# Turning the feed-forward activations on VectorE instead of TensorE

## The chip, the cores and the metric

The kernel runs on one core of one Trainium2 chip. The metric is the device time of one execution in microseconds (us), lower is better; the kernel before is given as the median of 3 executions. A core has TensorE (PE in the profile; PEld is its weight load), VectorE (DVE), ScalarE (ACT), GpSimd (POOL) and SyncE (SP), each with an instruction queue of its own, worked off in order.

## The reference, cut to what matters

The kernel computes one transformer layer for 256 latent tokens and 256 context tokens of width 2048: a modulated norm, a wide projection, two kinds of attention, an output projection, and a feed-forward part, all in float32. The change touches the last part alone:

```python
def swiglu_sublayer(x, shift, scale, gate, norm_g, w_ff_gate, w_ff_up, w_ff_down):
    h = modulate(rms_norm(x, norm_g), shift, scale)
    return x + gate * ((jax.nn.silu(h @ w_ff_gate) * (h @ w_ff_up)) @ w_ff_down)
```

The feed-forward width (DFF) is 5632 = 11 x 512.

## The kernel before

Every large product is made by one helper, `project`. It multiplies 256 tokens (two tiles `tk` of 128) by 512 weight columns and walks over the contraction in weight tiles of 2 x 128 rows. SyncE loads such a weight tile (`wraw`, 512 KB, seven buffers, L224). Float32 accuracy comes from splitting it into a rounded part and a rest: ScalarE casts it (`whi`, L231, three buffers), VectorE subtracts (`wlo`, L232, three buffers). TensorE then makes three matmuls for each of 2 x 2 pairs of row block and token tile (L236 with `whi`, L237 with `wlo`, L238 with `whi` and the rest of the activations): twelve matmuls of 512 columns a weight tile. `whi` and `wlo` of a tile can be made only when TensorE has finished the tile three before it.

`project` calls `tick()` and, if given, `side()` after every weight tile. `after(n, f)` puts `f` on a list that `tick()` counts down, so f runs some tiles later; `evac` is called when a token tile's sum is complete.

The feed-forward part has two stages. In gate/up, for each of 11 column groups `cg`, the gate projection (8 weight tiles) ends with a SiLU on ScalarE into `act[tk]`, and the up projection (8 more) ends with a multiplication into `act[tk]` on VectorE (L983, in place). The down stage multiplies `act` by `w_ff_down`, 22 weight tiles for each of 4 column groups. For that the activations have to stand transposed, as a split pair `fT`: TensorE turns `act[tk]` in four 128 x 128 pieces into PSUM (`ftp`, L990), then `split` casts (ScalarE, L241) and subtracts (VectorE, L242). From cg 2 on, two pieces of another vector (`ada`, L430/L432 on VectorE, 512 KB loaded each) are taken after each projection.

A scheduling layer settles the order of each queue when the program is built; the code gives the dependences and a first order.

Of the kernel before, what the change touches and what calls it, by code (L numbers as in the profile page):

```python
# [17 lines left out]
P = 128  # L18
D = 2048
NKT = D // P  # L20
# [14 lines left out]
CG = 512  # L35
# [5 lines left out]
TURN = 3  # L41
TURN2 = 5
# [3 lines left out]
def hybrid_block(ctx: ExitStack, tc: tile.TileContext, t: dict, out: bass.AP):  # L46
    nc = tc.nc
# [9 lines left out]
    def big_tile(name, dt=F32):  # L57
        return big.tile([P, 2048], dt, tag="big", name=name)

    def mm_ps(name="mm"):  # L60
        return psum.tile([P, CG], F32, tag="mm", bufs=4, name=name)

    def tp_ps(name="tp"):
        return psum.tile([P, CG], F32, tag="tp", bufs=2, name=name)
# [4 lines left out]
    def scratch(name, n=CG, dt=F32, tag="scr", bufs=3):  # L69
        return scr.tile([P, n], dt, tag=tag, bufs=bufs, name=name)  # L70
# [5 lines left out]
    ident = tab.tile([P, P], F32, name="ident")  # L76
# [145 lines left out]
    def load_w(src, r0, c0, nk=WK, in_big=False):  # L222
        raw = wp.tile([P, WK, CG], F32, tag="wraw", bufs=WRAW, name="wraw")
        nc.sync.dma_start(out=raw[:, 0:nk], in_=src[r0:r0 + nk * P, c0:c0 + CG].rearrange("(k p) c -> p k c", p=P))  # L224
        if in_big:
            both = big_tile("wbig", F32R).rearrange("p (h k c) -> p h k c", h=2, c=CG)
            hi, lo = both[:, 0], both[:, 1]
        else:
            hi = wp.tile([P, WK, CG], F32R, tag="whi", bufs=WHI, name="whi")
            lo = wp.tile([P, WK, CG], F32R, tag="wlo", bufs=WLO, name="wlo")  # L230
        last_hi.append(nc.scalar.copy(out=hi[:, 0:nk], in_=raw[:, 0:nk]))  # L231
        last_lo.append(nc.vector.tensor_tensor(out=lo[:, 0:nk], in0=raw[:, 0:nk], in1=hi[:, 0:nk].bitcast(F32), op=ALU.subtract))  # L232
        return hi, lo

    def mm3(ps, ah, al, wh, wl, first, last):
        nc.tensor.matmul(ps, lhsT=ah, rhs=wh, start=first, stop=False)  # L236
        nc.tensor.matmul(ps, lhsT=ah, rhs=wl, start=False, stop=False)  # L237
        return nc.tensor.matmul(ps, lhsT=al, rhs=wh, start=False, stop=last)  # L238

    def split(hi, lo, src):  # L240
        nc.scalar.copy(out=hi, in_=src)  # L241
        nc.vector.tensor_tensor(out=lo, in0=src, in1=hi.bitcast(F32), op=ALU.subtract)  # L242
# [178 lines left out]
    def ada_pieces(a, chunk):  # L421

        for kt, hf in [(kt, hf) for kt in range(NKT) for hf in range(2)]:
            wt = wp.tile([P, 1024], F32, tag="wraw", bufs=WRAW, name="wada2")
            nc.sync.dma_start(out=wt, in_=w_ada[kt * P:(kt + 1) * P, chunk * D + hf * 1024: chunk * D + (hf + 1) * 1024])
            dst = a[:, hf * 1024:(hf + 1) * 1024]
            yield None
            with tc.issue_after(last_lo[-1].ins):
                if kt == 0:
                    nc.vector.tensor_scalar(out=dst, in0=wt, scalar1=sc[:, 0, 0:1], scalar2=None, op0=ALU.mult)  # L430
                else:
                    nc.vector.scalar_tensor_tensor(out=dst, in0=wt, scalar=sc[:, 0, kt:kt + 1], in1=dst, op0=ALU.mult, op1=ALU.add)  # L432
# [94 lines left out]
    def take(gen, n):  # L527
        for _ in range(n):
            if next(gen, gen) is gen:
                return  # L530

    def drain(gen):
        for _ in gen:
            pass
# [9 lines left out]
    def after(n, fn):  # L544
        late.append([n, fn])

    def tick():
        for e in list(late):
            e[0] -= 1
            if e[0] <= 0:  # L550
                late.remove(e)
                e[1]()
# [61 lines left out]
    def project(src, hl, nkt, c0, evac, kt0=0, side=None, head=1, tail=1, hook=None):  # L614


        ps = [mm_ps() for _ in range(2)]
        nt = nkt // WK
        order = [(i, tk) for i in range(nt) for tk in range(2)]
        order[:2 * head] = [(i, tk) for tk in range(2) for i in range(head)]  # L620
        order[-2 * tail:] = [(i, tk) for tk in range(2) for i in range(nt - tail, nt)]
        wt = {}
        for n, (i, tk) in enumerate(order):
            if i not in wt:
                wt[i] = load_w(src, i * WK * P, c0, in_big=WHI <= i < head or nt - tail <= i < nt - WHI)
            wh, wl = wt[i]
            for j in range(WK):
                k = i * WK + j
                ah, al = hl.at(kt0 + k, tk * P, P)
                mm3(ps[tk], ah, al, wh[:, j], wl[:, j], k == 0, k == nkt - 1)  # L630
            if i == nt - 1 and (tail > 1 or tk == 1):
                for x in ([tk] if tail > 1 else range(2)):
                    evac(x, ps[x])
            if hook:
                hook(i, tk)
            if n % 2:
                tick()
                if side:
                    side()
                yield None  # L640
# [24 lines left out]
    def q_evac(qT, br):  # L665
        def f(tk, ps):
            o = norm_rope(ps, br, "q", tk)

            def turn():
                tp = tp_ps("qtp")  # L670
                for h in range(4):
                    nc.tensor.transpose(out=tp[:, h * P:(h + 1) * P], in_=o[:, h * P:(h + 1) * P], identity=ident)
                src = tp.rearrange("p (h q) -> p h q", h=4)
                split(qT[:, 0, :, tk * P:(tk + 1) * P], qT[:, 1, :, tk * P:(tk + 1) * P], src)
            after(5 + tk, turn)
        return f
# [79 lines left out]
    def unit(br, u):  # L756
        return (u // 4, u % 4) if br == "a" else (u // 8, u // 2 % 4)
# [59 lines left out]
    for n, (br, u) in enumerate(units):  # L817
        q = (br, unit(br, u)[0])
# [33 lines left out]
    for cg in range(4):  # L852
# [19 lines left out]
        def gated(tk, ps):  # L872
            g = gs[tk]
            nc.vector.tensor_tensor(out=g, in0=ps, in1=g, op=ALU.mult)
            nc.vector.tensor_tensor(out=m[tk], in0=m[tk], in1=g, op=ALU.add)
            after(2 + tk, turn(tk))

        def turn(tk, cg=cg, m=m):
            def f():
                tp = tp_ps("mtp")  # L880
                for j in range(4):
                    nc.tensor.transpose(out=tp[:, j * P:(j + 1) * P], in_=m[tk][:, j * P:(j + 1) * P], identity=ident)
                hi, lo = mT.four(cg, tk * P, P)
                split(hi, lo, tp.rearrange("p (h q) -> p h q", h=4))
            return f
# [34 lines left out]
    hT = Parts("hT", NKT)  # L920
# [49 lines left out]
    w_g, w_u, w_d = t["w_ff_gate"][0], t["w_ff_up"][0], t["w_ff_down"][0]  # L970
    NFT = DFF // P
    fT = Parts("fT", NFT)
    for cg in range(DFF // CG):
        if cg == 2:
            a5 = big_tile("ada5")
            a5_gen = ada_pieces(a5, 5)
        act = [scratch(f"act{tk}") for tk in range(2)]

        def g_evac(tk, ps):
            nc.scalar.activation(out=act[tk], in_=ps, func=AF.Silu)  # L980

        def u_evac(tk, ps):
            nc.vector.tensor_tensor(out=act[tk], in0=ps, in1=act[tk], op=ALU.mult)  # L983
            after(2 + tk, turn(tk))

        def turn(tk, cg=cg, act=act):
            def f():
                tp = tp_ps("ftp")
                for j in range(4):
                    nc.tensor.transpose(out=tp[:, j * P:(j + 1) * P], in_=act[tk][:, j * P:(j + 1) * P], identity=ident)  # L990
                hi, lo = fT.four(cg, tk * P, P)
                split(hi, lo, tp.rearrange("p (h q) -> p h q", h=4))
            return f

        drain(project(w_g, hT, NKT, cg * CG, g_evac, **(dict(head=TURN2, hook=head_hook) if cg == 0 else {})))
        if cg > 1:
            take(a5_gen, 2)
        drain(project(w_u, hT, NKT, cg * CG, u_evac))
        if cg > 1:
            take(a5_gen, 2)  # L1000
    drain(a5_gen)
# [2 lines left out]
    for cg in range(4):  # L1004
        def d_evac(tk, ps):
            xr = scratch("xr2", tag="p", bufs=4)
            nc.gpsimd.dma_start(out=xr, in_=x2_d[tk, :, cg * CG:(cg + 1) * CG])
            y = scratch("y")
            nc.vector.tensor_tensor(out=y, in0=ps, in1=a5[:, cg * CG:(cg + 1) * CG], op=ALU.mult)
            nc.vector.tensor_tensor(out=y, in0=y, in1=xr, op=ALU.add)  # L1010
            (nc.sync if cg == 3 else nc.gpsimd).dma_start(out=out[0, tk * P:(tk + 1) * P, cg * CG:(cg + 1) * CG], in_=y)
        drain(project(w_d, fT, NFT, cg * CG, d_evac, tail=TURN if cg == 3 else 1))


_INS = ["x", "c", "ctx", "c_ctx", "w_ada", "b_ada", "norm1_g", "w_in", "q_norm_a", "k_norm_a", "q_norm_b", "k_norm_b",
# [35 lines left out]
```

## Time and profile before

| what | value |
|---|---|
| median of 3 executions | 1725.93 us (1722.39 to 1726.39) |
| the profiled execution, its own time | 1727.13 us |
| span from first to last instruction in it | 1725.0 us |
| TensorE busy | 1697.9 us, 98% |
| VectorE busy | 1134.0 us, 66% |
| ScalarE busy | 772.9 us, 45% |
| granted TensorE clock, mean | 0.999 |

A busy TensorE is not TensorE at its peak, since matmuls overlap; what matters is the time from one start to the next. In the groups of the profile a row gives line, engine, operation, what is written from what, shapes and count, then busy us and mean ns of one, then the idle time before it. In rows in order of time stand the start, the length (from the first start to the last end where several are merged), and in brackets how long the engine idled before and what ended that. In the waits stand the waiting engine and line, what it waited for, the total, the count and the longest.

### The profile page before, as it was taken

How to read it: one execution, taken by the hardware profiler on the slowest of the kernel's cores; microseconds unless marked ns; L12 is line 12 of the kernel's file. 1: busy time of each engine (PE TensorE's matmuls, PEld its weight loads, DVE VectorE, ACT ScalarE, POOL GpSimd, SP SyncE). 2: the span in 40 equal slices, each digit the busy share in tenths (PEclk: the TensorE clock that was granted, in tenths of full speed). 3: DMA queues.
4: the chain of work that ended last, by engine and by line, in shares of the span. 5: the costliest groups of instructions: out<-in, count | busy, mean ns of one | idle time of the engine just before them, and what ended most of it. 6: DMA issues, size and time to landing. Idle time of an engine off the chain costs nothing.

```text
span 1725.0 us, 21768 instructions
## 1 busy us (share of the span) xinstructions
PE 1697.9 (98%) x8110; PEld 1370.6 (79%) x8110; DVE 1134.0 (66%) x1444; ACT 772.9 (45%) x1064; POOL 134.1 (8%) x204
## 2 busy tenths in 40 slices
PE   7999999999999999999999999999999999999998
PEld 5676778877887788887888788888888888888887
DVE  4764779788788979786665754565556565444554
ACT  5221223245666565666544444444444444333332
POOL 2100002011131120002111100000000000000000
PEclk9999999999999999999999999999999999999999
DMA  9987694778756667777787756677777777666662
GB/s 275 314 303 266 238 328 163 222 243 267 248 177 216 224 221 263 225 232 243 253 314 227 228 182 194 208 231 234 241 234 241 234 241 229 210 209 200 219 206 87
DMA packets 192873, 400.82 MB, mean 232 GB/s; under 512 B 13600, under 2 KB 25968, under 8 KB 192256
## 3 DMA queue, kind: packets, MB, share of 16 engines
q1 hardware_dynamic: 184816, 372.86, 66.3%
q0 software_dynamic: 7952, 26.58, 4.9%
q8 instruction: 63, 1.03, 0.2%
q14 instruction: 42, 0.34, 0.1%
HBM read 388.87 MB, written 10.52 MB: 232 GB/s over the span
## 4 chain that ended last, share of the span: by engine, by line
PE 85%; DVE 5%; issue 3%; DMA 3%; ACT 1%; POOL 1%; SPq 1%; ACTq 0%; DVEq 0%; POOLq 0%
PE mm L237 26%; PE mm L236 26%; PE mm L238 26%; DMA wraw<-in_w_in_dram 3%; DVE wlo L232 2%; PE ptp L726 1%; PE ada L292 1%; ACT whi L231 1%; PE o L744 1%; PE ftp L990 1%; PE s L706 1%; PE o L237 0%; PE o L238 0%; PE o L236 0%; PE s L236 0%
## 5 line engine op out<-in xcount | busy, mean ns | idle before, releaser
L232 DVE TENSOR_TENSOR wlo<-wraw,whi 128x1024 fp32r<-128x1024 f32 (+1 forms) x506 | 611.3, 1210 | 465.1 <-ACT whi L231 461.6
L231 ACT CAST whi<-wraw 128x1024 fp32r<-128x1024 f32 (+1 forms) x506 | 527.4, 1043 | 790.1 <-PE mm L238 657.6
L237 PE MATMUL mm<-wlo,hT 128*128 128x512 f32 x696 | 271.2, 390 | 2.0 <-DVE wlo L232 2.0
L236 PE MATMUL mm<-whi,hT 128*128 128x512 f32 x696 | 273.1, 392 | 0.0
L238 PE MATMUL mm<-whi,hT 128*128 128x512 f32 x696 | 271.6, 390 | 0.1
L236 PE MATMUL mm<-whi,xT 128*128 128x512 f32 x640 | 255.9, 403 | 1.4 <-DVE vb L415 0.9
L237 PE MATMUL mm<-wlo,xT 128*128 128x512 f32 x640 | 251.2, 392 | 1.0 <-DVE wlo L232 0.9
L238 PE MATMUL mm<-whi,xT 128*128 128x512 f32 x640 | 250.3, 391 | 0.0
L237 PEld LDWEIGHTS mm<-wlo,hT 128*128 128x128 f32 x696 | 130.9, 188 | 28.9 <-DVE wlo L232 2.4
L238 PEld LDWEIGHTS mm<-whi,hT 128*128 128x128 f32 x696 | 130.8, 188 | 28.0 <-DVE hT L242 0.5
L432 DVE SCALAR_TENSOR_TENSOR ada<-wada,sc,ada 128x1024 f32<-128x1024 f32 x120 | 151.9, 1276 | 0.0
L236 PEld LDWEIGHTS mm<-whi,xT 128*128 128x128 f32 x640 | 119.5, 188 | 40.7 <-issue 11.4
L236 PEld LDWEIGHTS mm<-whi,hT 128*128 128x128 f32 x696 | 130.8, 188 | 26.3
L237 PEld LDWEIGHTS mm<-wlo,xT 128*128 128x128 f32 x640 | 120.4, 188 | 26.9 <-DVE wlo L232 3.3
L238 PEld LDWEIGHTS mm<-whi,xT 128*128 128x128 f32 x640 | 120.1, 188 | 25.8 <-DVE xT L382 0.4
L236 PE MATMUL mm<-whi,fT 128*128 128x512 f32 x352 | 137.2, 390 | 0.0
L238 PE MATMUL mm<-whi,fT 128*128 128x512 f32 x352 | 137.0, 389 | 0.0
L237 PE MATMUL mm<-wlo,fT 128*128 128x512 f32 x352 | 136.9, 389 | 0.0
L236 PEld LDWEIGHTS mm<-whi,fT 128*128 128x128 f32 x352 | 66.1, 188 | 14.5 <-issue 0.8
L238 PEld LDWEIGHTS mm<-whi,fT 128*128 128x128 f32 x352 | 66.1, 188 | 13.9
L237 PEld LDWEIGHTS mm<-wlo,fT 128*128 128x128 f32 x352 | 66.1, 188 | 13.4
L236 PE MATMUL mm<-whi,cT 128*128 128x512 f32 x192 | 75.0, 393 | 1.4 <-ACT cT L381 1.4
(246 smaller groups left out, 2092.0 us busy)
## 6 DMA issues: line engine op xcount, KB each, us to landing
wada<-in_w_ada_dram SPq DMA_DIRECT2D x192, 512.0 KB, 4.8
wraw<-in_w_in_dram SPq DMA_DIRECT2D x154, 512.0 KB, 4.8
wraw<-in_w_ff_gate_dram SPq DMA_DIRECT2D x88, 512.0 KB, 4.3
wraw<-in_w_ff_up_dram SPq DMA_DIRECT2D x88, 512.0 KB, 3.7
wraw<-in_w_ff_down_dram SPq DMA_DIRECT2D x88, 512.0 KB, 4.2
wraw<-in_w_br_a_dram SPq DMA_DIRECT2D x32, 512.0 KB, 5.1
wraw<-in_w_out_dram SPq DMA_DIRECT2D x32, 512.0 KB, 5.8
wraw<-in_w_br_b_dram SPq DMA_DIRECT2D x16, 512.0 KB, 5.9
```

What stands on the lines that cost most here:

```text
L231: last_hi.append(nc.scalar.copy(out=hi[:, 0:nk], in_=raw[:, 0:nk]))
L232: last_lo.append(nc.vector.tensor_tensor(out=lo[:, 0:nk], in0=raw[:, 0:nk], in1=hi[:, 0:nk].bitcast(F32), op=ALU.subtract))
L236: nc.tensor.matmul(ps, lhsT=ah, rhs=wh, start=first, stop=False)
L237: nc.tensor.matmul(ps, lhsT=ah, rhs=wl, start=False, stop=False)
L238: return nc.tensor.matmul(ps, lhsT=al, rhs=wh, start=False, stop=last)
L292: last_pe[0] = nc.tensor.matmul(aps[32 * g:32 * g + 32, 0:ncol], lhsT=cst[:, k, :], rhs=rhs, start=(k < 4), stop=(k >= NKT - 4))
L432: nc.vector.scalar_tensor_tensor(out=dst, in0=wt, scalar=sc[:, 0, kt:kt + 1], in1=dst, op0=ALU.mult, op1=ALU.add)
L706: nc.tensor.matmul(sps[i], lhsT=qT[rows, x, hh, tk * P:(tk + 1) * P], rhs=kT["b", grp][y][rows, hh, :], start=(n == 0), stop=(n == 2))
L726: nc.tensor.transpose(out=tp[:, kt * P:(kt + 1) * P], in_=p[:, kt * P:(kt + 1) * P], identity=ident)
L744: nc.tensor.matmul(op[:, 0:BV], lhsT=pT[:, kt, :], rhs=vb[:, kt, hh * BV:(hh + 1) * BV], start=(kt == 0), stop=(kt == 3))
L990: nc.tensor.transpose(out=tp[:, j * P:(j + 1) * P], in_=act[tk][:, j * P:(j + 1) * P], identity=ident)
```

## The change

After the up projection, `act[tk]` is no longer turned by TensorE. A generator `turned` issues sixteen VectorE transposes, each from 32 partitions (four 32 x 32 blocks) of `act[tk]` to another 32 partitions of a scratch tile `fturn` in SBUF; together they give the four 128 x 128 transposes. The hook `blocks_turned` runs after each weight tile of the feed-forward projections and takes four steps of the generator at the head of `chain`. When a tile's sixteen are issued, `after(4, ...)` puts off its split by four weight tiles; the split reads `fturn` instead of PSUM.

```diff
+    chain = []
+    def blocks_turned():
+        for _ in range(4):
+            if chain and next(chain[0], chain) is chain:
+                chain.pop(0)
+    def turned(src, dst_hi, dst_lo):
+        whole = scratch("fturn", tag="sq", bufs=2)
+        sv = src.rearrange("p (k b j) -> p b k j", k=4, b=4)
+        dv = whole.rearrange("p (k a j) -> p a k j", k=4, a=4)
+        for a in range(4):
+            for b in range(4):
+                nc.vector.transpose(out=dv[32 * b:32 * b + 32, a], in_=sv[32 * a:32 * a + 32, b])
+                yield None
+        after(4, lambda: split(dst_hi, dst_lo, whole.rearrange("p (k q) -> p k q", k=4)))
...
         def u_evac(tk, ps):
             nc.vector.tensor_tensor(out=act[tk], in0=ps, in1=act[tk], op=ALU.mult)
-            after(2 + tk, turn(tk))
-
-        def turn(tk, cg=cg, act=act):
-            def f():
-                tp = tp_ps("ftp")
-                for j in range(4):
-                    nc.tensor.transpose(out=tp[:, j * P:(j + 1) * P], in_=act[tk][:, j * P:(j + 1) * P], identity=ident)
-                hi, lo = fT.four(cg, tk * P, P)
-                split(hi, lo, tp.rearrange("p (h q) -> p h q", h=4))
-            return f
+            chain.append(turned(act[tk], *fT.four(cg, tk * P, P)))
...
-        drain(project(w_u, hT, NKT, cg * CG, u_evac))
+        drain(project(w_u, hT, NKT, cg * CG, u_evac, side=blocks_turned))
```

The gate and the down projections get the same `side=blocks_turned`.

The order of the queues shows what that becomes. VectorE before, from the evacuation of one column group's up projection on (act_10211 and act_10212 are its two token tiles; wlo x2 stands for two weight tiles):

```order
L983 TENSOR_TENSOR act_10211<-mm,act_10211 128x512
L983 TENSOR_TENSOR act_10212<-mm,act_10212 128x512
L232 TENSOR_TENSOR wlo<-wraw,whi 128x1024 x2
L242 TENSOR_TENSOR fT_10563<-ftp,fT_10563 128x4x128
L232 TENSOR_TENSOR wlo<-wraw,whi 128x1024
L242 TENSOR_TENSOR fT_10563<-ftp,fT_10563 128x4x128
L232 TENSOR_TENSOR wlo<-wraw,whi 128x1024 x3
```

The same place on VectorE in the changed kernel (its line 1002 is the evacuation, 988 the transpose):

```order
L988 STREAM_TRANSPOSE fturn<-act_10289 32x4x32 x12
L232 TENSOR_TENSOR wlo<-wraw,whi 128x1024
L988 STREAM_TRANSPOSE fturn<-act_10289 32x4x32 x4
L232 TENSOR_TENSOR wlo<-wraw,whi 128x1024
L988 STREAM_TRANSPOSE fturn<-act_10290 32x4x32 x3
L232 TENSOR_TENSOR wlo<-wraw,whi 128x1024
L988 STREAM_TRANSPOSE fturn<-act_10290 32x4x32 x7
L232 TENSOR_TENSOR wlo<-wraw,whi 128x1024
L988 STREAM_TRANSPOSE fturn<-act_10290 32x4x32 x5
L242 TENSOR_TENSOR fT_10625<-fturn,fT_10625 128x4x128
L232 TENSOR_TENSOR wlo<-wraw,whi 128x1024
L988 STREAM_TRANSPOSE fturn<-act_10290 32x4x32
```

Twelve transposes now stand ahead of the first weight split after the evacuation, and the other twenty lie between the next ones; one fT subtraction, wlo and the ada pieces follow. ScalarE before, between two SiLU evacuations (the ten weight tiles of whi x10 end with the fourth of the next gate projection):

```order
L231 CAST whi<-wraw 128x1024 x10
L241 CAST fT_10563<-ftp 128x4x128
L231 CAST whi<-wraw 128x1024
L241 CAST fT_10563<-ftp 128x4x128
L231 CAST whi<-wraw 128x1024 x5
```

And in the changed kernel:

```order
L231 CAST whi<-wraw 128x1024 x10
L241 CAST fT_10625<-fturn 128x4x128
L231 CAST whi<-wraw 128x1024 x3
L241 CAST fT_10625<-fturn 128x4x128
L231 CAST whi<-wraw 128x1024 x3
```

The first cast of `fT` keeps its place; the second moves behind two more weight tiles, and both now wait for VectorE's transposes where they waited for TensorE's.

More of the change, by code (lines that the diff above doesn't have):

```diff
@@ L983, in u_evac @@
             nc.vector.tensor_tensor(out=act[tk], in0=ps, in1=act[tk], op=ALU.mult)
-            after(2 + tk, turn(tk))
-        def turn(tk, cg=cg, act=act):
-            def f():
-                tp = tp_ps("ftp")
-                for j in range(4):
-                    nc.tensor.transpose(out=tp[:, j * P:(j + 1) * P], in_=act[tk][:, j * P:(j + 1) * P], identity=ident)
-                hi, lo = fT.four(cg, tk * P, P)
-                split(hi, lo, tp.rearrange("p (h q) -> p h q", h=4))
-            return f
-        drain(project(w_g, hT, NKT, cg * CG, g_evac, **(dict(head=TURN2, hook=head_hook) if cg == 0 else {})))
+            chain.append(turned(act[tk], *fT.four(cg, tk * P, P)))
+        drain(project(w_g, hT, NKT, cg * CG, g_evac, side=blocks_turned, **(dict(head=TURN2, hook=head_hook) if cg == 0 else {})))
         if cg > 1:
             take(a5_gen, 2)
-        drain(project(w_u, hT, NKT, cg * CG, u_evac))
+        drain(project(w_u, hT, NKT, cg * CG, u_evac, side=blocks_turned))
         if cg > 1:
@@ L1011, in d_evac @@
             (nc.sync if cg == 3 else nc.gpsimd).dma_start(out=out[0, tk * P:(tk + 1) * P, cg * CG:(cg + 1) * CG], in_=y)
-        drain(project(w_d, fT, NFT, cg * CG, d_evac, tail=TURN if cg == 3 else 1))
+        drain(project(w_d, fT, NFT, cg * CG, d_evac, side=blocks_turned, tail=TURN if cg == 3 else 1))
 _INS = ["x", "c", "ctx", "c_ctx", "w_ada", "b_ada", "norm1_g", "w_in", "q_norm_a", "k_norm_a", "q_norm_b", "k_norm_b",
```

## The prediction

> **What bounds the kernel now.** I read the page first (busy times, chain, groups), then the feed-forward stage by stretches, its waits, and one group of 512 columns in order of time on TensorE, VectorE and ScalarE.
>
> ```profile
> span 1725.0 us, 21768 instructions
> PE 1697.9 (98%) x8110; PEld 1370.6 (79%) x8110; DVE 1134.0 (66%) x1444; ACT 772.9 (45%) x1064; POOL 134.1 (8%) x204
> PE mm L237 26%; PE mm L236 26%; PE mm L238 26%; DMA wraw<-in_w_in_dram 3%; DVE wlo L232 2%; PE ptp L726 1%; PE ada L292 1%; ACT whi L231 1%; PE o L744 1%; PE ftp L990 1%; PE s L706 1%; PE o L237 0%; PE o L238 0%; PE o L236 0%; PE s L236 0%
> ```
>
> The chain is TensorE's, and the transposes of the feed-forward activations (ftp, L990) stand in it. Next, one stretch of the gate/up stage, and the two largest waits of its engines from 1040 to 1480 us (total, times, longest):
>
> ```profile
> core 0: us, PE busy (x) PEld busy (x) DVE busy (x) ACT busy (x) POOL busy (x), PEclk, DMA share, GB/s
> 1170.00:1215.00 45.00, 45.00 (x205) 37.32 (x204) 26.60 (x24) 19.47 (x21) 0.00 (x0) 1.00 0.73 238
> ```
> ```profile
> ACT whi L231 <- PE mm L238: 243.0, 149, 1.7
> DVE wlo L232 <- ACT whi L231: 186.9, 143, 2.0
> ```
>
> TensorE is busy for 45.00 of 45.00 us at the full granted clock. VectorE is busy for 26.60 and waits for ScalarE, which waits for TensorE to hand back a weight buffer. So TensorE is the bound there, and work that leaves it is a gain as long as VectorE, which is to take the work over, still has the next weights ready in time.
>
> **What the change removes.** TensorE, in order of time:
>
> ```profile
> 1160.17 0.39 PE L236 MATMUL mm<-whi,hT 128*128 128x512 f32 x1
> ...
> 1166.97 0.39 PE L236 MATMUL mm<-whi,hT 128*128 128x512 f32 x1
> ...
> 1169.46 0.39 PE L238 MATMUL mm<-whi,hT 128*128 128x512 f32 x1
> 1169.69 0.60 PE L990 MATMUL ftp<-ident,act 128*128 128x128 f32 x4
> 1170.05 0.47 PE L236 MATMUL mm<-whi,hT 128*128 128x512 f32 x1
> 1170.36 0.39 PE L237 MATMUL mm<-wlo,hT 128*128 128x512 f32 x1
> ```
>
> From 1160.17 to 1166.97 there are 30 matmuls, 0.227 us from start to start; a weight tile is twelve of them, 2.72 us. From 1169.46 to 1170.36 are two such intervals, 0.45, that took 0.90: four transposes cost 0.45 us of the path. There are two groups of four for each 512 columns, and 11 times 512 columns: 22 x 0.45 = 9.9 us, which is the whole gain.
>
> **What the change adds.** 22 tiles times sixteen are 352 VectorE instructions of 32 partitions x 128 elements. The two halves of each split stay, with another source, which I cost at nothing: both engines had the room shown above. The queues of SyncE and GpSimd keep the same rows in the same order. No row shows such a transpose, so its price p, from one start to the next, is bounded by near rows. The first two come from the groups of the first 20 us (busy us, mean ns), the others are VectorE in order of time:
>
> ```profile
> L380 DVE TENSOR_SCALAR hx<-xtp,mod,mod 128x128 f32<-128x128 f32 x1 | 0.4, 404 | 0.0
> L108 DVE TENSOR_TENSOR ce<-ce,cin 32x128 f32<-32x128 f32 x1 | 0.3, 280 | 0.0
> ```
> ```profile
> 14.04 0.17 DVE L304 TENSOR_REDUCE mod<-atp 128x2 f32<-128x8 f32 x1
> 14.24 0.16 DVE L307 TENSOR_TENSOR mod<-mod,vt 128x2 f32<-128x2 f32 x1
> ...
> 18.48 0.29 DVE L382 TENSOR_TENSOR xT<-hx,xT 128x128 fp32r<-128x128 f32 x1
> 18.69 0.68 DVE L141 SCALAR_TENSOR_TENSOR junk<-tok 128x512 f32<-128x512 f32 x1
> ```
>
> Low end 0.21: the 128-element L382 is 0.29 long, but its successor starts after 0.21, over its tail. High end 0.40, L380's length. Between them, the row of the very shape, L108, is 0.28 long, and where an instruction cannot run over the tail of the one before (L307 needs L304's result) it starts 0.03 after that one's end: 0.28 + 0.03 = 0.31. I take 0.31, because each of the sixteen writes to another quarter of the partitions than the one before it, and every pair of rows here that overlaps stays on the same partitions; I do not grant that overlap where no row shows it.
>
> [...]
>
> **What lies behind the added work.** VectorE and ScalarE at the same place as above:
>
> ```profile
> 1165.54 1.23 DVE L232 TENSOR_TENSOR wlo<-wraw,whi 128x1024 fp32r<-128x1024 f32 x1 [0.69 <-ACT whi L231]
> 1166.68 1.28 DVE L983 TENSOR_TENSOR act<-mm,act 128x512 f32<-128x512 f32 x2
> 1168.26 1.23 DVE L232 TENSOR_TENSOR wlo<-wraw,whi 128x1024 fp32r<-128x1024 f32 x1 [0.30 <-ACT whi L231]
> ...
> 1172.12 0.68 DVE L242 TENSOR_TENSOR fT<-ftp,fT 128x512 fp32r<-128x512 f32 x1
> ```
> ```profile
> 1161.24 2.47 DVE L432 SCALAR_TENSOR_TENSOR ada<-wada,sc,ada 128x1024 f32<-128x1024 f32 x2
> ```
> ```profile
> 1167.17 1.06 ACT L231 CAST whi<-wraw 128x1024 fp32r<-128x1024 f32 x1 [1.67 <-PE mm L238]
> 1169.89 1.05 ACT L231 CAST whi<-wraw 128x1024 fp32r<-128x1024 f32 x1 [1.67 <-PE mm L238]
> 1170.85 0.58 ACT L241 CAST fT<-ftp 128x512 fp32r<-128x512 f32 x1
> ```
>
> Call the up projection's last weight tile L; L+1 starts at 1166.97, my zero. wlo of L+1 and L+2 stand before the evacuation (act), which ends at 0.99; the one at 1168.26 is L+3's. Without transposes L+3 starts at 5.44 and its second matmul reads wlo: wanted by 5.67, and 2.72 later for each tile after. In the changed order VectorE has 12 transposes first, then wlo L+3, 4, L+4, 3, L+5, 7, L+6, 5 and a split, L+7, 1 and a split, L+8, then in nine of the eleven cycles two ada pieces, L+9. On ScalarE the second cast of fT now stands ahead of whi L+8, so that one waits for the last transpose too. With wlo 1.23 long (1.14 to a successor on the same partitions), a split 0.60, two ada 2.38 from start to successor, and p = 0.31:
> - L+3: 0.99 + 12p + 1.23 = 5.94, wanted 5.67: 0.27 late.
> - L+4 ends 8.41, L+5 10.48, L+6 13.88: each wanted later, by 8.66, 11.38, 14.10.
> - L+7 starts at 0.99 + 31p + 3 x 1.23 + 1.14 + 0.60 = 16.03 and ends 17.26; wanted 16.82 + 0.27: 0.17 late.
> - L+8: last transpose done at 17.57, cast 18.15, whi 19.20, wlo 20.43; wanted 19.54 + 0.17 = 19.71: 0.72 late.
> - L+9: 19.20 + 1.14 + 2.38 + 1.23 = 23.95; wanted 21.99 + 1.16 = 23.15: 0.80 late.
> - L+10 has slack again: 25.09 against 26.67.
>
> So a cycle with ada loses 0.27 + 0.17 + 0.72 + 0.80 = 1.96 and gains 0.90: +1.06, nine times; the other two lose 1.16: +0.26 each. 9.5 + 0.5 = +10 us. The same walk gives +3 at p = 0.29, +17 at 0.33, -4 at 0.27, and the whole -9.9 from 0.25 down: the balance lies near 0.28. SyncE's weight loads wait for wlo too and would be issued up to 3 us later:
>
> ```profile
> wraw<-in_w_ff_gate_dram SPq DMA_DIRECT2D x88, 512.0 KB, 4.3
> ```
>
> With seven load buffers, the load that waits for wlo of L+3 is that of L+10 (L+8 where two ada pieces lie between), whose cast is due at 19.2 (13.8): 5.94 + 4.3 is before both, so I cost that at nothing.
>
> The profiled execution took 1727.13 us around its span of 1725.0, 1.2 above the median of 1725.93. 1727.1 + 10 = 1737.1 on its scale, 1736 on the median's.
>
> **Rivals.**
> - Overlapping transposes: p of 0.21 to 0.25, every wlo in time, 1725.9 - 9.9 = 1716. For it: the L382 row, and VectorE's 18 idle us in each 45. Against it: the change of partitions. This is the other side, decided by whether p is below 0.28.
> - A price at the balance, 0.25 to 0.29: stalls and gain cancel, 1720 to 1729.
> - A dearer transpose, as L380's 0.40 would have it: 0.09 x 32 = 2.9 us more a cycle, 11 cycles, about 1768. Against it: L380 reads per-partition scalars and PSUM, the transposes neither.
> - That TensorE's time is not freed, because it would wait anyway: against it, its 45.00 of 45.00 us.
>
> **How the numbers follow.** A change of 0.3%, 5.2 us, is about what a measurement of this kernel can tell from none. Overlap, 0.33, nearly all of it faster by more than that; the balance and the lower edge of my forecast, 0.20, same; the forecast 0.37 and the dearer case 0.10, slower by more. The time is the forecast's, 1736, with a range of its own from 1729 to 1743 (p from 0.29 to 0.33). Both signs hold chance, so the range for 8 in 10 goes from the whole gain, 1715, to a p of about 0.345, 1748; the remainder of the dearer case is left out.
>
> **What would show it.** Right: no ftp rows on TensorE; the transposes spaced by about 0.31; TensorE waiting for wlo at the third, seventh, eighth and ninth tile behind each evacuation, some 2 us a cycle, and ScalarE's whi waiting behind the cast of fT. Wrong: starts 0.21 to 0.25 apart and no wait of TensorE for wlo in the gate/up stage. The price of one transpose decides it.

## The result, and the profile after

The changed kernel takes 1737.61 us (median of 6, 1735.70 to 1739.15) against 1725.43 for the kernel before (6, 1722.39 to 1726.83): ratio 1.0074, 95% interval 1.0063 to 1.0084. It is 12.2 us slower; 1736 was forecast. Of all the runs compared below, one took 1980.16 us at a granted clock of 0.804, where the others had 0.998 to 1.000; it belongs to the kernel with three transposes a tile, not pinned, and is left out of its median.

The page of the changed kernel, the lines that answer to those of before (span; busy times; the chain by line):

```profile
span 1735.0 us, 21943 instructions
PE 1699.4 (98%) x8022; PEld 1359.4 (78%) x8022; DVE 1237.3 (71%) x1796; ACT 772.3 (45%) x1064; POOL 134.0 (8%) x204
PE mm L237 22%; PE mm L238 22%; PE mm L236 22%; DVE wlo L232 6%; DVE fturn L988 5%; DMA wraw<-in_w_in_dram 2%; PE ada L292 1%; ACT whi L231 1%; PE ptp L726 1%; PE o L744 1%; DVE act L1002 1%; PE s L706 1%; DVE fT L242 0%; PE o L237 0%; PE o L238 0%
```

TensorE's 88 transposes are gone (8110 instructions to 8022) and VectorE's 352 have come (1444 to 1796). The chain now runs through VectorE: `wlo` 6% where it had 2%, and the transposes, `fturn`, 5%. The busy share of TensorE, 98% both times, tells nothing of this.

The group of the new tile (with the shortest, median and longest of one in ns, and the first and last start), and of the waits from 1040 to 1490 us the three largest that did not exist before (total, times, longest):

```profile
L988 DVE STREAM_TRANSPOSE fturn<-act x352: 289/303/308, 1031.3 to 1505.0; 32x128 f32<-32x128 f32 x176
```
```profile
ACT fT L241 <- DVE fturn L988: 82.6, 19, 5.3
PEld mm L237 <- DVE wlo L232: 25.6, 36, 0.9
PE mm L237 <- DVE wlo L232: 10.4, 36, 0.5
```

A transpose is 303 ns long. TensorE waited at 36 matmuls for a rest part of the weights (`wlo`); before, such a wait is not among those of this stage at all. One cycle of VectorE in order of time, the place that the prediction walked through:

```profile
1166.47 1.28 DVE L1002 TENSOR_TENSOR act<-mm,act 128x512 f32<-128x512 f32 x2
1167.67 3.76 DVE L988 STREAM_TRANSPOSE fturn<-act 32x128 f32<-32x128 f32 x12
1171.46 1.22 DVE L232 TENSOR_TENSOR wlo<-wraw,whi 128x1024 fp32r<-128x1024 f32 x1
...
1182.46 0.69 DVE L242 TENSOR_TENSOR fT<-fturn,fT 128x512 fp32r<-128x512 f32 x1
1183.07 1.22 DVE L232 TENSOR_TENSOR wlo<-wraw,whi 128x1024 fp32r<-128x1024 f32 x1
1184.32 0.31 DVE L988 STREAM_TRANSPOSE fturn<-act 32x128 f32<-32x128 f32 x1
1185.31 0.69 DVE L242 TENSOR_TENSOR fT<-fturn,fT 128x512 fp32r<-128x512 f32 x1 [0.69 <-ACT fT L241]
1186.26 1.22 DVE L232 TENSOR_TENSOR wlo<-wraw,whi 128x1024 fp32r<-128x1024 f32 x1 [0.26 <-ACT whi L231]
```

From 1167.67 to 1171.46 lie twelve transposes: 0.316 us from start to start. From there to 1186.26 VectorE idles only for the cast of fT and for the `whi` queued behind that cast. TensorE in the same cycle:

```profile
1172.20 0.39 PE L236 MATMUL mm<-whi,hT 128*128 128x512 f32 x1
1172.74 0.50 PE L237 MATMUL mm<-wlo,hT 128*128 128x512 f32 x1 [0.15 <-DVE wlo L232]
1173.08 0.40 PE L238 MATMUL mm<-whi,hT 128*128 128x512 f32 x1
...
1183.54 0.39 PE L236 MATMUL mm<-whi,hT 128*128 128x512 f32 x1
1184.34 0.50 PE L237 MATMUL mm<-wlo,hT 128*128 128x512 f32 x1 [0.41 <-DVE wlo L232]
...
1186.97 0.39 PE L236 MATMUL mm<-whi,hT 128*128 128x512 f32 x1
1187.54 0.50 PE L237 MATMUL mm<-wlo,hT 128*128 128x512 f32 x1 [0.18 <-DVE wlo L232]
...
1190.17 0.39 PE L236 MATMUL mm<-whi,hT 128*128 128x512 f32 x1
1191.07 0.50 PE L237 MATMUL mm<-wlo,hT 128*128 128x512 f32 x1 [0.52 <-DVE wlo L232]
```

1172.20 is the start of L+3. Its second matmul starts 0.54 us after the first instead of 0.23, and the third 0.34 after that: 0.42 lost. The same pattern stands at three more tiles of the cycle: the second matmul comes 0.80 us after the first at 1183.54 (L+7), 0.57 at 1186.97 (L+8), 0.90 at 1190.17 (L+9), each time with 0.34 to the next. With 0.23 as the undisturbed step the four cost 0.42 + 0.68 + 0.45 + 0.78 = 2.33 us. The stage holds ten such cycles; the eleventh falls in the down stage. In seven of the ten, two ada pieces stand ahead of the `wlo` of L+9. The first cycle has no piece there and the second and the tenth have one; in these three L+9 is not late, and about 1.5 us are lost.

### The profile page after: what moved, and what is told of

Same layout as the page of the kernel before. It is cut to its first block, busy times and chain, and to the rows that moved or that the text cites. A ratio compares the mean times of both kernels' runs of the same rounds, so it can differ in the third digit from the quotient of the medians.

```text
span 1735.0 us, 21943 instructions
## 1 busy us (share of the span) xinstructions
PE 1699.4 (98%) x8022; PEld 1359.4 (78%) x8022; DVE 1237.3 (71%) x1796; ACT 772.3 (45%) x1064; POOL 134.0 (8%) x204
## 4 chain that ended last, share of the span: by engine, by line
PE 73%; DVE 17%; issue 5%; DMA 2%; ACT 2%; POOL 1%; SPq 0%; DVEq 0%; ACTq 0%; POOLq 0%
PE mm L237 22%; PE mm L238 22%; PE mm L236 22%; DVE wlo L232 6%; DVE fturn L988 5%; DMA wraw<-in_w_in_dram 2%; PE ada L292 1%; ACT whi L231 1%; PE ptp L726 1%; PE o L744 1%; DVE act L1002 1%; PE s L706 1%; DVE fT L242 0%; PE o L237 0%; PE o L238 0%
## 5 line engine op out<-in xcount | busy, mean ns | idle before, releaser
L237 PE MATMUL mm<-wlo,hT 128*128 128x512 f32 x696 | 275.7, 396 | 12.6 <-DVE wlo L232 10.6
L236 PE MATMUL mm<-whi,hT 128*128 128x512 f32 x696 | 271.4, 390 | 0.0
L236 PE MATMUL mm<-whi,xT 128*128 128x512 f32 x640 | 255.9, 403 | 1.3 <-DVE vb L415 0.7
L236 PEld LDWEIGHTS mm<-whi,hT 128*128 128x128 f32 x696 | 130.7, 188 | 27.7
L236 PEld LDWEIGHTS mm<-whi,xT 128*128 128x128 f32 x640 | 119.5, 188 | 40.6 <-issue 11.5
L236 PE MATMUL mm<-whi,fT 128*128 128x512 f32 x352 | 137.1, 389 | 0.0
L988 DVE STREAM_TRANSPOSE fturn<-act 32x128 f32<-32x128 f32 x352 | 106.4, 302 | 5.3
L236 PEld LDWEIGHTS mm<-whi,fT 128*128 128x128 f32 x352 | 66.1, 188 | 14.7 <-issue 0.8
```

What stands on the lines that cost most here:

```text
L988: nc.vector.transpose(out=dv[32 * b:32 * b + 32, a], in_=sv[32 * a:32 * a + 32, b])
```

## The experiments

All times are medians; "before" was run on the same chips, and lay at 1724.9 to 1725.0.

**No turning at all.** The split reads `act` directly, five and nine tiles later:

```diff
-            chain.append(turned(act[tk], *fT.four(cg, tk * P, P)))
+            hi, lo = fT.four(cg, tk * P, P)
+            after(5 + 4 * tk, lambda src=act[tk]: split(hi, lo, src.rearrange("p (k q) -> p k q", k=4)))
```

> Neither engine turns the activations: the split reads act as it stands, so the turning itself is left out of the computation. Theory A (TensorE's 22 groups cost 0.45 us each on the path, and the changed kernel gives that back and more through late weight splits): 9.9 us below the kernel before, about 1716, and no wait of TensorE for wlo in the gate/up stage. Rival (the removed transposes were worth less, since TensorE would have waited anyway): 1722 or more.

1714.33 us, ratio 0.9935 (0.9920 to 0.9950), 10.6 us below before, and no wait of TensorE for `wlo` in the stage. TensorE's transposes were worth what they seemed to be. The length of the stage can be read off one row of each trace, the matmuls of L236 on hT (first and last start), of the kernel before, the changed kernel and this one:

```profile
L236 PE MATMUL mm<-whi,hT x696: 387/389/628, 983.9 to 1477.5; 128*128 128x512 f32 x174
```
```profile
L236 PE MATMUL mm<-whi,hT x696: 387/389/477, 980.7 to 1487.2; 128*128 128x512 f32 x174
```
```profile
L236 PE MATMUL mm<-whi,hT x696: 388/389/481, 983.8 to 1466.8; 128*128 128x512 f32 x174
```

Gate/up takes 493.6, 506.5 and 483.0 us. The changed kernel is 12.9 longer there than the kernel before, about as much as the medians differ (12.2). The stages ahead differ by some 4 us from trace to trace without order (in the traces of all these kernels this stage starts at 979.8 to 983.9).

**Blocks left on their own partitions.** The same sixteen instructions, each reading and writing one quarter, which changes after every fourth:

```diff
-        for a in range(4):
-            for b in range(4):
-                nc.vector.transpose(out=dv[32 * b:32 * b + 32, a], in_=sv[32 * a:32 * a + 32, b])
+        for b in range(4):
+            for a in range(4):
+                nc.vector.transpose(out=dv[32 * b:32 * b + 32, a], in_=sv[32 * b:32 * b + 32, a])
```

> As the changed kernel, but each of the sixteen instructions reads and writes the same 32 partitions, which change only after every fourth instruction; the blocks so stay on their own partitions, that is, the move between the quarters is left out. Theory A (an instruction that starts on other partitions than the last one cannot run over its tail): three of four start 0.21 to 0.24 us apart and the fourth 0.31, 0.25 on average, few late weight splits, 1716 to 1721. Rival B (a transpose takes 0.31 us from start to start whatever its partitions): spacing 0.31 and 1737, as the changed kernel.

1713.25 us, ratio 0.9931 (0.9915 to 0.9946). VectorE in order of time:

```profile
1161.41 2.66 DVE L988 STREAM_TRANSPOSE fturn<-act 32x128 f32<-32x128 f32 x12
1164.10 1.23 DVE L232 TENSOR_TENSOR wlo<-wraw,whi 128x1024 fp32r<-128x1024 f32 x1
...
1167.43 0.68 DVE L988 STREAM_TRANSPOSE fturn<-act 32x128 f32<-32x128 f32 x3
1168.05 1.17 DVE L232 TENSOR_TENSOR wlo<-wraw,whi 128x1024 fp32r<-128x1024 f32 x1
```

Three that stay on one quarter take 0.62 us, 0.207 each; twelve with their changes of quarter 2.69, 0.224 each, where the changed kernel takes 3.79. Number, shape and order relative to the weights are the same, so the price is not that of the instruction as such, and Rival B falls. What this kernel leaves open is whether the change from one instruction to the next costs, or the crossing from one quarter to another, which it leaves out as well; the pairs below decide that.

**The loops exchanged.** `for b` outside, `for a` inside, the instruction itself unchanged: four in a row write one quarter, and each reads another one than the last.

> As the changed kernel with the two loops over the blocks exchanged: four instructions in a row now write the same 32 partitions, and read from a new quarter each time. The whole turning is done. Theory A1 (a change of quarter on either side forbids the overlap): spacing 0.31, 1737. Theory A2 (only a change of the quarter written does): three of four 0.21 to 0.24, and 1716 to 1721. Rival B (the length is inherent): 1737, told from A1 by the kernel in which blocks stay on their own quarter.

1736.30 us, ratio 1.0064 (1.0047 to 1.0080), and the same burst of twelve:

```profile
1167.28 3.77 DVE L988 STREAM_TRANSPOSE fturn<-act 32x128 f32<-32x128 f32 x12
1171.09 1.23 DVE L232 TENSOR_TENSOR wlo<-wraw,whi 128x1024 fp32r<-128x1024 f32 x1
```

3.81 for twelve, 0.318 each. A change on the reading side alone is enough, so exchanging the loops does not help: A1.

**Both token tiles turned together.** Every move from quarter to quarter is made for both tiles one after the other, two such pairs a weight tile, so still four instructions (the setting up of the two tiles is left out here):

```diff
-        for _ in range(4):
+        for _ in range(2):
...
-                nc.vector.transpose(out=dv[32 * b:32 * b + 32, a], in_=sv[32 * a:32 * a + 32, b])
+                for tk in range(2):
+                    nc.vector.transpose(out=dv[tk][32 * b:32 * b + 32, a], in_=sv[tk][32 * a:32 * a + 32, b])
...
+        for tk in range(2):
+            after(3 + tk, lambda tk=tk: split(*dsts[tk], whole[tk].rearrange("p (k q) -> p k q", k=4)))
```

> As the changed kernel at four transposes a weight tile, but the two token tiles are turned together: each move from one quarter to another is made for both tiles one after the other, so every second instruction stays on the quarters of the one before. The whole turning is done. Theory A (only a change of quarter costs the overlap): starts 0.315 and 0.207 us apart in turn, 0.26 on average; L+3's wlo ends at 5.35, wanted by 5.67, none late, about 1714. Rival (any such sequence runs at 0.31): 1736.

1713.45 us, ratio 0.9937 (0.9921 to 0.9952):

```profile
1163.61 3.02 DVE L989 STREAM_TRANSPOSE fturn<-act 32x128 f32<-32x128 f32 x12
1166.66 1.23 DVE L232 TENSOR_TENSOR wlo<-wraw,whi 128x1024 fp32r<-128x1024 f32 x1
```

3.05 us for twelve, 0.254 each on average, where 0.26 was expected; how that divides between the first and the second of a pair the merged row does not show. The 32 transposes of this cycle make the moves of the changed kernel in another order, 24 of them from one quarter to another, and their bursts take 8.25 us up to what follows them, 0.258 each; in the changed kernel's cycle the bursts with 31 of the 32 take 9.88, 0.319 each. So it is the change from one instruction to the next that costs, and not the crossing. TensorE does not wait for a `wlo` anywhere in the stage. The whole turning is done, and the change is now a gain. The price, 0.06 us less an instruction, is not the only difference from the changed kernel, though: all 32 transposes lie ahead of the `wlo` of L+7 here, and both fT subtractions behind it. That the price alone is enough is shown by the kernel with own quarters, which kept the order and ran at 0.224.

**Three a tile, pinned.** The price stays; the work is laid between more weight splits:

```diff
-        for _ in range(4):
+        for _ in range(3):
...
-                nc.vector.transpose(out=dv[32 * b:32 * b + 32, a], in_=sv[32 * a:32 * a + 32, b])
+                with tc.issue_after(last_lo[-1].ins):
+                    nc.vector.transpose(out=dv[32 * b:32 * b + 32, a], in_=sv[32 * a:32 * a + 32, b])
```

> As the changed kernel, but three transposes a weight tile instead of four, each pinned behind the weight split last emitted, so that 9 and then 3 a tile lie between the weight splits, over eleven tiles. The price of one stays 0.31. Theory A (the loss comes from VectorE's backlog within eight tiles, not from the work as such): L+3's wlo ends 5.1 us behind the evacuation's tile, wanted at 5.7, and no later one is late: the whole gain, about 1716. Rival C (the 352 instructions slow the matmuls or the other engines wherever they stand): about 1737, with slower matmuls or waits elsewhere.

1711.89 us (1711.26 to 1712.81), ratio 0.9923 (0.9909 to 0.9938): 13.0 us below before. This is the lowest median of the versions that do the whole turning, but its interval overlaps that of the pairs. The same stretch of the stage, 1040 to 1460 us, in the kernel before, the changed one and this one (PE, PEld, DVE, ACT, POOL busy, clock, DMA share, GB/s):

```profile
1040.00:1460.00 420.00, 420.00 (x1890) 347.83 (x1889) 243.02 (x220) 179.64 (x191) 2.03 (x4) 1.00 0.72 230
```
```profile
1040.00:1460.00 420.00, 410.05 (x1762) 327.53 (x1760) 324.84 (x515) 171.33 (x182) 0.00 (x0) 1.00 0.68 223
```
```profile
1040.00:1460.00 420.00, 420.00 (x1855) 347.77 (x1854) 339.93 (x528) 183.09 (x194) 2.03 (x4) 1.00 0.75 235
```

VectorE is busier than in the changed kernel, 339.93 of 420 us, at the same 303 ns each, and TensorE does not wait: it is the backlog ahead of single weight splits that cost, not the load. (The splits of fT wait for the last transpose of their tile and so move later with it.) Rival C falls. Its gate/up stage takes 483.0 us (L236 from 979.8 to 1462.8), as long as without any turning; what else lies between these two kernels falls in the stages ahead, and their intervals overlap.

**Three a tile, not pinned.** Only the first line of that edit.

> As the changed kernel with three transposes a weight tile and nothing pinned: the scheduling layer then puts 9, 3, 6, 8, 5 and 1 between the weight splits, so all 32 still lie ahead of L+8's. Theory A (what counts is VectorE's work ahead of each weight split, 0.315 us a transpose): L+6, L+7, L+8 and L+9 late by some 2.2 us a cycle, about 1736. Rival D (the number a tile in the code is what made the spread kernel fast): about 1714.

1737.15 us, ratio 1.0076 (1.0053 to 1.0099). TensorE's waits from 1040 to 1480 us are nearly those of the changed kernel:

```profile
PEld mm L237 <- DVE wlo L232: 26.8, 36, 0.9
PE mm L237 <- DVE wlo L232: 11.6, 36, 0.5
```

The second matmul is late at L+6 to L+9 (steps of 0.65, 0.78, 0.56 and 0.91 us in one cycle). The number in the code did not matter, because the scheduling layer drew the transposes forward again, to 9, 3, 6, 8, 5 and 1 between the weight splits as expected; rival D falls.

**The splits of fT pinned later.** Casts and subtractions of fT are made six tiles after the transposes, each behind the weight split last emitted there:

```diff
-        after(4, lambda: split(dst_hi, dst_lo, whole.rearrange("p (k q) -> p k q", k=4)))
+        def late_split():
+            wv = whole.rearrange("p (k q) -> p k q", k=4)
+            with tc.issue_after(last_hi[-1].ins):
+                nc.scalar.copy(out=dst_hi, in_=wv)
+            with tc.issue_after(last_lo[-1].ins):
+                nc.vector.tensor_tensor(out=dst_lo, in0=wv, in1=dst_hi.bitcast(F32), op=ALU.subtract)
+        after(6, late_split)
```

> As the changed kernel, but the two splits of fT are made six weight tiles after the transposes and pinned there, so that no cast of fT stands ahead of the whi of L+5 to L+9 on ScalarE, and no fT subtraction ahead of their wlo. Theory A (of the loss per cycle, L+3 is owed to the twelve transposes in front, L+7 to L+9 to the casts and subtractions on top): only L+3 is late, 0.33 us and 0.11 for restarting; 0.44 lost, 0.96 gained, -5.7 us, about 1719. Rival E (the transposes alone make the loss, the place of the splits does not matter): 1733 or more.

1723.52 us, ratio 0.9990 (0.9980 to 0.9999): 14 us less than the changed kernel, but 4.5 more than expected. TensorE's waits:

```profile
PEld mm L237 <- DVE wlo L232: 10.8, 19, 0.6
```

19 instead of 36. In a cycle L+3 (step 0.55) and L+7 (0.52, then 0.34) are still late, L+8 and L+9 no more. The expectation had L+7 in time; it is 0.29 late and costs another 0.11 for the wider step behind it: 0.4 x 11 = 4.4 us, about the miss. Rival E falls too. So the place of the splits explains L+8 and L+9, the transposes L+3 and, here, where 32 of them and no split stand ahead of it, L+7. With 0.43 + 0.40 lost and 0.93 gained a cycle comes out nearly even, as measured.

## Why the prediction was right, point by point

- **The gain.** 9.9 us were forecast; the kernel without turning lay 10.6 below before (8.6 to 13.8 by its interval). In the trace of before L+1 starts at 1166.97 and L+4 at 1176.06, 9.09 us for 36 matmuls that take 8.16 undisturbed: 0.465 a group, since the matmuls behind a group keep a wider step for a while (ten steps from 1173.55 take 2.29 us instead of 2.27). That is 10.2 for 22. Of the 10.6 us by which the stage is shorter in the trace without turning, 1.2 lie in its first weight tiles, for which no cause was sought.
- **The price.** 0.31 was taken, 0.316 measured. Its two parts were less near: 0.28 long and 0.03 to the next start were taken, 0.303 and 0.013 were measured, and the two errors nearly cancel. The ground for granting no overlap, that a change of partitions loses it, is shown by three kernels: 0.207 without a change, 0.254 with every second one changing, 0.318 when the side that is read changes each time. The low end of the range, 0.21, was the price of an instruction that stays.
- **The late tiles.** L+3, L+7, L+8 and L+9 were named, and these four are late. The walk has a slip: 16.82, the time at which L+7 is wanted, already holds the 0.27 of L+3, and 0.27 is added to it once more. Put right, L+7 is 0.44 late and L+8 0.45, and the sum stays 1.96. So the walk says 0.27, 0.44, 0.45 and 0.80; measured are 0.42, 0.68, 0.45 and 0.78, together 2.33. Two things made the sum larger. VectorE ends the `wlo` of L+7 at 1183.07 + 1.22, 17.53 us behind the start of L+1 in that trace (1166.76), where the walk has 17.26: the transposes came at 0.316 and small gaps around the weight splits were left out. And the step from a late matmul to the next is 0.34 instead of 0.23, 0.11 that the walk left out. At L+7 and L+8 that only makes the next tile wanted later, since VectorE's queue does not wait for TensorE there; behind the last late tile it is a loss of its own.
- **The sum.** The kernel with own quarters, which has the same first weight tiles and no late ones, takes 484.3 us for the stage, the changed kernel 506.5: 22.2 lost in ten cycles. The late tiles account for it: seven cycles with 2.33 and three with 1.5 are 20.8, and steps a little wider behind each late matmul (twelve with no other late one among them take 2.74 to 2.78 us instead of 2.72) make up about the rest. The eleventh cycle loses about 1.1 more in the down stage. That is 23.3 lost, where the walk came to 20.0 (9 x 1.96 + 2 x 1.16); the changed kernel lies as much above the one without turning, 23.3. Against a gain of 10.2 this leaves 13.1; the medians say 12.2, the forecast was 10.
- **What was luck.** The walk had VectorE some 0.3 us early from L+7 on and left out the wider step: some 5 us too little in all. It also counted two ada pieces ahead of L+9 in nine cycles, and only seven have two of them at that place: 2 x 0.80 = 1.6 us too much. The two errors partly offset each other. The mechanism and the tiles were right; that the total came within some 2 us was in part chance.
- **What was costed at nothing.** From 1040 to 1480 us ScalarE waited for TensorE (160.2 us before `whi`, 15.4 before the SiLU) and for VectorE's transposes (82.6 before the cast of `fT`), and for no weight load, so SyncE's loads did cost nothing. The cast of `fT` takes 0.62 us from SBUF where it took 0.58 from PSUM, the subtraction 0.69 where it took 0.68; only the place of the splits in the queues mattered, and the walk had that.
- **The rivals.** Overlapping transposes gave 1713 to 1714 where they were made to happen (1716 forecast), so that case was sized about right and its condition not met. The price at the balance, 0.25 to 0.29, was touched at its lower edge only: the pairs, at 0.254 and in a somewhat different order, gave the whole gain. No other run has a price between that and 0.316. The dearer transpose is ruled out by the measured 0.316, and a TensorE whose time would not be freed by the kernel without turning.

## What to carry to other kernels

Work moved off the bounding engine was free here only where the receiving queue met each single due time: sum the queue's work ahead of every operand that the bounding engine waits for, tile by tile, and not the busy share; here a VectorE busy for 340 us of 420 cost nothing when its work was spread, and one busy for 325 of 420 cost 22 us over the stage when it was bunched. After building, read the order that the scheduling layer made, as the same edit with and without pinning lay 25 us apart. Where short VectorE instructions move data between partition quarters, put those with the same pair of quarters next to each other (here 0.254 us an instruction instead of 0.316).

## What the runs showed of the hardware that I had not expected

- A change of the quarter that is read costs as much as a change of the one written: 0.318 against 0.316 us from start to start, 0.207 without either. The crossing from one quarter to another is not what costs: the same moves in pairs take 0.258 us each over a cycle, where the changed kernel takes 0.319.
- A matmul that waited for `wlo` is followed at 0.34 us instead of 0.23 (0.33 to 0.35 at the 36 of the changed kernel's stage), at a granted clock of 1.00, so that a delay of 0.29, as at L+7 with the later splits of fT, costs 0.40.
